# Expert weights in runs of 8192 bytes, with strided moving columns in the up product

## The chip, the cores and the metric

One core of a Trainium2 chip runs the whole program. The metric is the device time of one execution in microseconds; before the change its median over three runs is 1952.04 us (1950.11 to 1953.3).

## What is computed

The program computes four blocks over 256 tokens of 1024 features, in f32. The first block has two layers; each is a mixer (convolutions in the first, stick-breaking attention in the second), a layer norm, a mixture of experts and another layer norm. The second block (attention mixers and dense feed-forward parts) follows and is untouched here. The mixture of experts, which the change is about:

```python
g_logits = h @ rg_w + rg_b                   # 4 groups
grp = argmax(g_logits)
top_val, top_idx = top_k(e_logits[grp], 2)   # 2 of the group's 8 experts
weights = g_gate * softmax(top_val)
gate, up = split(rows_of_e @ w_up[e], 2)     # w_up[e]: 1024 x 1024
y = (silu(gate) * up) @ w_down[e]            # w_down[e]: 512 x 1024
out[tok] += y * weight
```

There are 32 experts in each of the two layers, and the kernel loads the weights of all of them: 4 MiB up and 2 MiB down for an expert.

## The kernel before

**The stages.** `tile_kernel` runs ten stages in order: convolutions (0), experts (1), stick-breaking attention (2), experts (3), and the second block (4 to 9). All weights are cut into items of at most 1 MiB, in the order of their use, in the list `items` (lines 125 to 176). `pump` (line 195) takes the next item as soon as a free buffer of 128 x 2048 f32 is usable for it and issues one DMA for it on SP's queue (line 205). `take` hands an item to its user, `done` gives the buffer back and pumps again. There are 7 buffers for all stages, 6 and 4 more while the first block runs, and 3 for the expert stages alone, so up to 20 items are under way or wait for TensorE when an expert stage begins. Items are loaded strictly in order: behind an expert stage's 192 items come those of the next mixer.

**An expert's items** (lines 137 to 143). The up weights are four items, the down weights two. `rows` (line 69) puts row 128 k + p of a matrix on partition p, at place k, and an item holds two places: on every partition two separate rows of 4096 bytes.

**The expert stage** (`moe`, from line 829). `router` picks the experts and leaves, for each token and expert, a place among 32 (`CAP`) in `rt["pos"]`. `gather_mm` (line 822) multiplies 128 features of `x` by a one-hot matrix, so that a group of tokens comes out with features on partitions; `gathered` brings the result through the layer norm's gain and bias (`put`, line 845) into `xgs`. The gain and bias stand on partitions in `fvec` (line 320), which `vector_loads` (line 322) makes by eight transposes. For expert e the loop then calls `up(e)`, `down(e - 1)` and `turn(e)`:

- `up` (line 882) has for each of its four items two places k, and for each of those four matmuls (j = 0 to 3). The stationary operand is the 32 gathered tokens, the moving one 256 columns of the weights: 128 gate columns and 128 up columns. Result j goes to partitions 32 j to 32 j + 31, so the four matmuls use the four column groups of the array. An f32 matmul leaves two records in the trace, so an up product has 8 x 4 x 2 = 64.
- `turn` (line 899) transposes the 32 x 512 hidden values, folded as 128 x 128, so that hidden units lie on partitions.
- `down` (line 906) does the same with the two down items, 32 records, and ScalarE copies the result out (line 921).

Every fourth expert `combine` (line 924) adds four experts' results into the accumulators. The next group of experts is gathered at places 5 and 6 of a group, and the first half of the first group inside `router`, ahead of the first up product.

Line 1658, in the attention of stage 7, multiplies the weights of a small compressor by `kps[n][:, :, l:l + 113:8]`: 75 moving columns with a step of eight elements. It is not changed.

Of the kernel before, what the change touches and what calls it, by code (L numbers as in the profile page):

```python
# [10 lines left out]
F32 = mybir.dt.float32  # L11
# [23 lines left out]
LN_MIX_G, LN_MIX_B, LN_FFN_G, LN_FFN_B, NORM = 0, 2, 4, 6, 8  # L35
# [33 lines left out]
def rows(ap):  # L69
    return ap.rearrange("(k p) n -> p k n", p=128)  # L70


@with_exitstack
def tile_kernel(ctx: ExitStack, tc: tile.TileContext, A, out, first=0, last=9):
    nc = tc.nc
    V, S, G, T, Q = nc.vector, nc.scalar, nc.gpsimd, nc.tensor, nc.sync
    NA, NB, NC, ND = 7, 6, 4, 3

    const = ctx.enter_context(tc.tile_pool(name="const", bufs=1))
# [7 lines left out]
    def bank():  # L87
        return psum.tile([128, 512], F32, name="ps", tag="ps")
# [4 lines left out]
    items, halves = [], []  # L93

    def dense(view, kind):
        items.append(view)
        i = len(items) - 1
        if kind in ("cols4", "cols2"):
            k = int(kind[4])
            n = 1024 // k  # L100
            for j in range(2):
                halves.append((i, (k, n), lambda t, j=j, k=k, n=n: t.rearrange("p (k n) -> p k n", k=k)
                               [:, :, j * n:(j + 1) * n]))
        elif kind == "feat":
            for m in range(2):
                halves.append((i, (8, 128), lambda t, m=m: t.rearrange("p (k n) -> p k n", k=8)
                               [:, :, m * 128:(m + 1) * 128]))
        elif kind == "gate":
            halves.append((i, (8, 112), lambda t: t[:, 0:896].rearrange("p (k n) -> p k n", k=8)))
        else:  # L110
            k, n = {"tok": (4, 256), "row": (1, 1024)}[kind]
            for j in range(2):
                halves.append((i, (k, n), lambda t, j=j, k=k: t[:, j * 1024:(j + 1) * 1024]
                               .rearrange("p (k n) -> p k n", k=k)))

    def cols(w, c0, n=256):
        return rows(w)[:, :, c0:c0 + n]

    def out_items(w, pairs=False):
        for j in range(0 if pairs else 2):  # L120
            dense(rows(w)[:, 0:4, j * 512:(j + 1) * 512], "cols4")
        for k in range(0 if pairs else 4, 8, 2):
            dense(rows(w)[:, k:k + 2, :], "cols2")
# [3 lines left out]
    for s in range(first, last + 1):  # L127
        stage_half[s] = len(halves)
        if s == 0:
            for i in range(2):  # L130
                dense(cols(A["even_w_in"][0], 2048 + 256 * i), "feat")
                dense(cols(A["even_w_in"][0], 1536 + 256 * i), "feat")
            for i in range(2):
                for c in (512, 1024, 0):
                    dense(cols(A["even_w_in"][0], c + 256 * i), "feat")
            out_items(A["even_w_out"][0])
        elif s in (1, 3):
            moe_items[s] = len(items)
            for e in range(NE):
                for k in range(4):  # L140
                    items.append(rows(A["expert_w_up"][s // 2, e])[:, 2 * k:2 * k + 2, :])
                for k in range(2):
                    items.append(rows(A["expert_w_down"][s // 2, e])[:, 2 * k:2 * k + 2, :])
        elif s == 2:
            for hg in range(4):
                dense(cols(A["odd_w_qkv"][0], 256 * hg), "feat")
                dense(cols(A["odd_w_qkv"][0], 1024 + 256 * hg), "feat")
                dense(cols(A["odd_w_qkv"][0], 2048 + 256 * hg), "tok")
            out_items(A["odd_w_o"][0])
        elif s == 4:  # L150
            for hg in range(4):
                for j in range(3):
                    dense(cols(A["w_in_ab_2"][0], (hg // 2) * 1536 + (hg % 2) * 256 + 512 * j), "tok")
            out_items(A["w_out_ab_2"][0], True)
        elif s in (5, 8):
            for f in range(NF + 1):
                if f < NF:
                    dense(cols(A["w_ffn_gate_2"][s // 7], 256 * f), "feat")
                    dense(cols(A["w_ffn_up_2"][s // 7], 256 * f), "feat")
                if f:  # L160
                    dense(rows(A["w_ffn_down_2"][s // 7])[:, 2 * f - 2:2 * f, :], "row")
        elif s in (6, 9):
            dense(rows(A["w_ple_proj_2"][s // 9]), "row")
            for u in range(4):
                dense(cols(A["w_ple_gate_2"][s // 9], 256 * u), "feat")
        else:
            w = A["w_in_nsa_2"][0]
            for j, n in enumerate(("k", "v")):
                dense(cols(w, 1024 + 256 * j), "tok")
            for n in ("k", "v"):  # L170
                items.append(A[f"cmp_{n}_w1_2"][0].rearrange("(l p) n -> p l n", p=128))
            for c in (1536, 2048):
                dense(cols(w, c), "tok")
            dense(cols(w, 2496, 112), "gate")
            for c in (0, 256, 1792, 2304, 512, 768):
                dense(cols(w, c), "tok")
            out_items(A["w_out_nsa_2"][0], True)
# [32 lines left out]
    def take(i):  # L210

        pump()
        t = raw[i]
        return t

    def done(i):
        if i not in taken:
            taken.add(i)
            free.append(where[i])
            pump()  # L220
# [75 lines left out]
    x = const.tile([128, 2, D], F32, name="x")  # L296
# [17 lines left out]
    ident = const.tile([128, 128], F32, name="ident")  # L314
# [4 lines left out]

    fvec = const.tile([128, 8, 14], F32, name="fvec")  # L320

    def vector_loads(vr):
        lo, hi = (0 if first < 4 else 8), (14 if last > 3 else 8)
        for j, n in enumerate(("ln_mix_g", "ln_mix_b", "ln_ffn_g", "ln_ffn_b", "norm_mix_2", "norm_ffn_2",
                               "norm_ple_2")):
            if lo <= 2 * j < hi:
                Q.dma_start(vr[2 * j:2 * j + 2, :], A[n])
        if lo:
            V.memset(vr[0:8, :], 0.0)

        def go():
            ps = bank()
            for k in range(8):
                T.transpose(ps[:, k * 14:k * 14 + hi], vr[0:hi, k * 128:(k + 1) * 128], ident[:hi, :hi])
            V.tensor_copy(fvec[:, :, 0:hi], ps[:, 0:112].rearrange("p (k n) -> p k n", k=8)[:, :, 0:hi])
        return go

    def fv(j):
        return lambda k: fvec[:, k, j:j + 1]
# [201 lines left out]
    def conv_mix():  # L541
        mp = rt["pool"]
        with tc.tile_pool(name="cm", bufs=1, reuse_waits="tile") as cp:
# [9 lines left out]
            Q.dma_start(fvr[36:37, :], A["even_norm_b_b"])  # L553
            pump(1)
            vectors = vector_loads(vr)
            prep = router_loads(0)
            pump()
# [165 lines left out]
    def router(mp):  # L723
# [59 lines left out]
        def first():  # L783
            place(0)
            warm(8)
            gather_mm(pg, 0, dsp[:, 0, 0:4])
# [35 lines left out]
    def gather_mm(ps, c, dsp):  # L822

        for k in range(8):
            T.matmul(ps[k // 4][:, k % 4 * 128:k % 4 * 128 + 128], x[:, c, k * 128:(k + 1) * 128],
                     dsp.rearrange("p e s -> p (e s)"), start=k % 4 == 0 and c == 0, stop=c == 1,
                     skip_group_check=True)

    def moe(layer):
        stage = 2 * layer + 1  # L830
        with tc.tile_pool(name="wd", bufs=ND, reuse_waits="tile") as wd, \
# [5 lines left out]
            router(mg)  # L837
            base = moe_items[stage]
            acc = [bank() for _ in range(4)]
            gain, bias = fv(LN_MIX_G + layer), fv(LN_MIX_B + layer)  # L840
            xgs, y4s, hts = {}, {}, {}
            dsp = rt["dt"][:, 0:512].rearrange("p (c e s) -> p c e s", c=2, e=8)
            dwt = rt["dt"][:, 512:].rearrange("p (q t) -> p q t", q=2)
# [38 lines left out]
            def up(e):  # L882
                g, el = divmod(e, 8)
                pu = bank()
                for kq in range(4):
                    i = base + 6 * e + kq
                    w = take(i).rearrange("p (k a j f) -> p k a j f", k=2, a=2, j=4)
                    for kk in range(2):
                        k = 2 * kq + kk
                        r = xgs[g][k // 4][:, k % 4, el * CAP:(el + 1) * CAP]  # L890
                        for j in range(4):
                            T.matmul(pu[32 * j:32 * j + 32, 0:256], r, w[:, kk, :, j, :], start=k == 0, stop=k == 7)  # L892
                    done(i)
                hs = mg.tile([128, 128], F32, name="hs")
                S.activation(hs, pu[:, 0:128], AF.Silu)  # L895
                V.tensor_tensor(out=hs, in0=hs, in1=pu[:, 128:256], op=OP.mult)  # L896
                hts[e] = hs
# [1063 lines left out]
    if 7 in stage_half:  # L1961
        j = halves[stage_half[7]][0]
# [51 lines left out]
```

## Time and profile before

| | |
|---|---|
| median of 3 runs | 1952.04 us |
| the profiled execution | 1952.0 us, span 1950.3 us |
| PE busy | 1638.0 us, 84% |
| PE weight loads busy | 1241.2 us, 64% |
| DVE, ACT, POOL busy | 40%, 35%, 10% |
| mean granted TensorE clock | 0.900 |
| DMA | 236570 packets, 559.04 MB, mean 287 GB/s |
| packets under 8 KB | 236408 |

Busy time is the union of an engine's instructions; matmuls are pipelined and their ends are modelled. The slices are fortieths of the span, 48.8 us each; a digit is the busy share in tenths. The DMA share is the mean busy share of the core's 16 DMA engines, and it can pass 1 where packets overlap. [...]

### The profile page before, as it was taken

The page shows a single profiled execution, that of the slowest core. Times are in us where ns is not written, and L with a number is a line of the kernel's source. Part 1 is how long each engine was busy: PE and PEld are TensorE (multiplying, and loading weights), DVE is VectorE, ACT ScalarE, POOL GpSimd, SP SyncE. Part 2 cuts the span into 40 slices and gives each one's busy share as a digit, 9 for nine tenths or more (in the row PEclk, how much of TensorE's full clock was granted, in tenths as well). Part 3 has the DMA queues.
Part 4 walks back from the last instruction along what each step waited for, and adds up shares of the span by engine and source line. Part 5 has one row for each costly group of instructions (what it writes and reads, how often), then busy time and mean ns, then how long its engine had stood idle before and what let it go on. Part 6 is the DMA issues. An engine that isn't in the chain of part 4 may idle for free. (4 is left out here: it accounts for less than half of the span.)

```text
span 1950.3 us, 34572 instructions
## 1 busy us (share of the span) xinstructions
PE 1638.0 (84%) x14717; PEld 1241.2 (64%) x14717; DVE 781.6 (40%) x1569; ACT 681.3 (35%) x1299; POOL 196.3 (10%) x152
## 2 busy tenths in 40 slices
PE   7769767667668999767657778999999998999998
PEld 7756423224226986323324225999999997799998
DVE  5873100001104663100001004666655857666557
ACT  3423111111114663211111114655444646654445
POOL 4721000000001000000000002111000412110001
PEclk9889878778878999977778788999999999999999
DMA  9549999999999659999999999545555463145550
GB/s 299 213 143 394 418 419 418 418 420 418 418 419 349 241 182 362 418 420 419 418 418 419 419 419 310 161 154 179 180 186 178 140 207 112 55 136 195 192 176 23
DMA packets 236570, 559.04 MB, mean 287 GB/s; under 512 B 15563, under 2 KB 124938, under 8 KB 236408
## 3 DMA queue, kind: packets, MB, share of 16 engines
q1 hardware_dynamic: 226520, 551.59, 74.3%
q10 hardware_dynamic: 9264, 4.97, 0.9%
q8 instruction: 119, 1.95, 0.4%
q14 instruction: 43, 0.35, 0.1%
q0 software_dynamic: 624, 0.18, 0.0%
HBM read 555.55 MB, written 1.15 MB: 285 GB/s over the span
## 5 line engine op out<-in xcount | busy, mean ns | idle before, releaser
L892 PE MATMUL ps<-w,xg 128*32 128x256 f32 x4096 | 362.3, 493 | 235.8 <-DMA w<-in_expert_w_up_dram 231.5
L892 PEld LDWEIGHTS ps<-w,xg 128*32 128x32 f32 x4096 | 134.7, 132 | 445.5 <-DMA w<-in_expert_w_up_dram 266.2
L251 DVE TENSOR_TENSOR wl<-w,wh 128x1024 fp32r<-128x1024 f32 x231 | 281.2, 1226 | 157.2 <-ACT wh L240 153.9
L240 ACT ACTIVATE wh<-w 128x1024 fp32r<-128x1024 f32 x273 | 283.5, 1051 | 90.5 <-PE ps L401 60.1
L896 DVE TENSOR_TENSOR hs<-hs,ps 128x128 f32<-128x128 f32 x64 | 18.4, 288 | 631.6 <-ACT hs L895 631.6
L400 PE MATMUL ps<-xh,wh 128*128 128x256 f32 (+1 forms) x840 | 237.1, 282 | 0.0
L402 PE MATMUL ps<-xh,wl 128*128 128x256 f32 (+1 forms) x840 | 236.3, 281 | 0.8 <-DVE wl L251 0.8
L401 PE MATMUL ps<-xl,wh 128*128 128x256 f32 (+1 forms) x840 | 236.6, 282 | 0.4 <-DVE xl L1218 0.3
L895 ACT ACTIVATE hs<-ps 128x128 f32<-128x128 f32 x64 | 17.8, 278 | 591.9 <-PE ps L892 587.2
L251 POOL TENSOR_TENSOR wl<-w,wh 128x1024 fp32r<-128x1024 f32 x42 | 115.5, 2764 | 996.2 <-ACT wh L240 996.2
L402 PEld LDWEIGHTS ps<-xh,wl 128*128 128x128 f32 (+1 forms) x840 | 159.2, 189 | 1.2 <-DVE wl L251 1.2
L401 PEld LDWEIGHTS ps<-xl,wh 128*128 128x128 f32 (+1 forms) x840 | 159.2, 189 | 1.2 <-DVE xl L1218 1.2
L400 PEld LDWEIGHTS ps<-xh,wh 128*128 128x128 f32 (+1 forms) x840 | 159.2, 190 | 0.0
L914 PE MATMUL ps<-w,ht 128*32 128x256 f32 x2048 | 144.9, 432 | 0.0
L921 ACT ACTIVATE y<-ps 32x256 f32<-32x256 f32 x256 | 96.0, 375 | 119.9 <-PE ps L914 113.8
L914 PEld LDWEIGHTS ps<-w,ht 128*32 128x32 f32 x2048 | 74.5, 128 | 67.6 <-issue 35.7
L402 PE MATMUL ps<-wh,xl 128*128 128x256 f32 x352 | 100.4, 285 | 5.0 <-DVE xl L1218 5.0
L400 PE MATMUL ps<-wh,xh 128*128 128x256 f32 x352 | 102.2, 290 | 1.5 <-ACT xh L1215 1.5
L401 PE MATMUL ps<-wl,xh 128*128 128x256 f32 x352 | 99.6, 283 | 0.0
L401 PE MATMUL ps<-al,wh 128*128 128x256 f32 x352 | 99.1, 281 | 0.0
L400 PE MATMUL ps<-ah,wh 128*128 128x256 f32 x352 | 99.0, 281 | 0.0
L402 PE MATMUL ps<-ah,wl 128*128 128x256 f32 x352 | 99.0, 281 | 0.0
(403 smaller groups left out, 2883.5 us busy)
## 6 DMA issues: line engine op xcount, KB each, us to landing
w<-in_expert_w_up_dram SPq DMA_DIRECT2D x256, 1024.0 KB
w<-in_expert_w_down_dram SPq DMA_DIRECT2D x128, 1024.0 KB
w<-in_w_ffn_gate_dram SPq DMA_DIRECT2D x22, 1024.0 KB
w<-in_w_ffn_up_dram SPq DMA_DIRECT2D x22, 1024.0 KB
w<-in_w_ffn_down_dram SPq DMA_DIRECT2D x22, 1024.0 KB
w<-in_odd_w_qkv_dram SPq DMA_DIRECT2D x12, 1024.0 KB
w<-in_w_in_ab_dram SPq DMA_DIRECT2D x12, 1024.0 KB
w<-in_w_in_nsa_dram SPq DMA_DIRECT2D x10, 1024.0 KB
```

The costliest lines, as they stand in the source:

```text
L240: S.activation(hv, src, AF.Copy)
L251: eng.tensor_tensor(out=lv, in0=src, in1=hv.bitcast(F32), op=OP.subtract)
L400: T.matmul(ps, lh, rh, start=start, stop=False, **kw)
L401: T.matmul(ps, lh, rl, start=False, stop=False, **kw)
L402: T.matmul(ps, ll, rh, start=False, stop=stop, **kw)
L892: T.matmul(pu[32 * j:32 * j + 32, 0:256], r, w[:, kk, :, j, :], start=k == 0, stop=k == 7)
L895: S.activation(hs, pu[:, 0:128], AF.Silu)
L896: V.tensor_tensor(out=hs, in0=hs, in1=pu[:, 128:256], op=OP.mult)
L914: T.matmul(pd[32 * c:32 * c + 32, 0:256], hts[e][:, 32 * j:32 * j + 32], w[:, jj, c * 256:(c + 1) * 256], start=j == 0, stop=j == 3)
L921: S.activation(y4s[q][32 * ee:32 * ee + 32, c * 256:(c + 1) * 256], pd[32 * c:32 * c + 32, 0:256], AF.Copy)
```

## The change

The expert weights are cut by a new view, `runs`, which puts rows 8 p to 8 p + 7 of an up matrix (4 p to 4 p + 3 of a down matrix) on partition p. An item still holds two places, but they are now adjacent in memory: one run of 8192 bytes on each partition. Three things follow from it. Feature 8 p + k of the tokens has to lie on partition p at place k, so `gather_mm` takes every eighth feature as its stationary operand, and the gain and bias are needed in that order too (`runvec`). And hidden unit 4 p + j has to lie on partition p for the down product, so the up product's result j takes every fourth column of the weights.

```diff
+def runs(ap):
+
+    return ap.rearrange("(p k) n -> p k n", p=128)
...
                 for k in range(4):
-                    items.append(rows(A["expert_w_up"][s // 2, e])[:, 2 * k:2 * k + 2, :])
+                    items.append(runs(A["expert_w_up"][s // 2, e])[:, 2 * k:2 * k + 2, :])
                 for k in range(2):
-                    items.append(rows(A["expert_w_down"][s // 2, e])[:, 2 * k:2 * k + 2, :])
+                    items.append(runs(A["expert_w_down"][s // 2, e])[:, 2 * k:2 * k + 2, :])
...
+    runvec = const.tile([128, 8, 4], F32, name="runvec") if first < 4 else None
...
             V.tensor_copy(fvec[:, :, 0:hi], ps[:, 0:112].rearrange("p (k n) -> p k n", k=8)[:, :, 0:hi])
+            if not lo:
+                ps = bank()
+                for k in range(8):
+                    T.transpose(ps[:, k * 4:k * 4 + 4], vr[0:4, k::8], ident[:4, :4])
+                V.tensor_copy(runvec.rearrange("p k n -> p (k n)"), ps[:, 0:32])
...
-            T.matmul(ps[k // 4][:, k % 4 * 128:k % 4 * 128 + 128], x[:, c, k * 128:(k + 1) * 128],
+            T.matmul(ps[k // 4][:, k % 4 * 128:k % 4 * 128 + 128], x[:, c, k::8],
...
-            gain, bias = fv(LN_MIX_G + layer), fv(LN_MIX_B + layer)
+            gain, bias = [lambda k, j=j + layer: runvec[:, k, j:j + 1] for j in (LN_MIX_G, LN_MIX_B)]
...
-                    w = take(i).rearrange("p (k a j f) -> p k a j f", k=2, a=2, j=4)
+                    w = take(i).rearrange("p (k a f j) -> p k a j f", k=2, a=2, j=4)
```

## Rows read from the trace of the kernel before

**Rows 1.** The page's 40 slices: busy tenths, granted clock, DMA share, rate.

```profile
PE   7769767667668999767657778999999998999998
...
PEclk9889878778878999977778788999999999999999
DMA  9549999999999659999999999545555463145550
GB/s 299 213 143 394 418 419 418 418 420 418 418 419 349 241 182 362 418 420 419 418 418 419 419 419 310 161 154 179 180 186 178 140 207 112 55 136 195 192 176 23
```

**Rows 2.** Windows; columns as in the first line, x counts instructions.

```profile
core 0: us, PE busy (x) PEld busy (x) DVE busy (x) ACT busy (x) POOL busy (x), PEclk, DMA share, GB/s
...
175.00:592.00 417.00, 298.06 (x3153) 137.30 (x3151) 35.44 (x102) 63.00 (x173) 3.46 (x6) 0.80 1.03 418
181.00:186.00 5.00, 5.00 (x96) 2.85 (x88) 0.44 (x2) 1.41 (x5) 0.00 (x0) 1.00 1.02 415
700.00:745.00 45.00, 45.00 (x308) 37.02 (x306) 28.06 (x67) 18.84 (x31) 1.10 (x2) 1.00 0.67 248
745.00:1183.00 438.00, 311.33 (x3374) 148.14 (x3377) 40.57 (x125) 72.33 (x192) 0.00 (x0) 0.81 1.02 416
```

**Rows 3.** Waits, 175 to 592 and 745 to 1183 us: total us, times, longest.

```profile
PE ps L892 <- DMA w<-in_expert_w_up_dram: 113.2, 92, 5.1
...
PE ps L892 <- DMA w<-in_expert_w_up_dram: 117.8, 93, 6.0
```

**Rows 4.** Timeline from 300 us: start, length, engine, line, operation, idle time before.

```profile
300.24 1.94 PE L892 MATMUL ps<-w,xg 128*32 128x256 f32 x16 [0.46 <-DMA w<-in_expert_w_up_dram]
300.67 0.20 PEld L892 LDWEIGHTS ps<-w,xg 128*32 128x32 f32 x4 [0.23 <-issue]
301.10 0.20 PEld L892 LDWEIGHTS ps<-w,xg 128*32 128x32 f32 x4 [0.23 <-issue]
...
302.81 1.69 PE L892 MATMUL ps<-w,xg 128*32 128x256 f32 x16 [0.63 <-DMA w<-in_expert_w_up_dram]
```

**Rows 5.** Timeline from 181 us, where an expert's weights had landed.

```profile
180.75 3.66 PE L892 MATMUL ps<-w,xg 128*32 128x256 f32 x64
...
184.23 1.91 PE L914 MATMUL ps<-w,ht 128*32 128x256 f32 x32
```

**Rows 6.** DMA issues of the page.

```profile
w<-in_expert_w_up_dram SPq DMA_DIRECT2D x256, 1024.0 KB
w<-in_expert_w_down_dram SPq DMA_DIRECT2D x128, 1024.0 KB
```

**Rows 7.** DMA view: 622 to 626, 526.0 to 526.5, 300 to 301 us; packets, MB, share.

```profile
DMA packets 1524, 1.54 MB, mean 386 GB/s; under 512 B 16, under 2 KB 1524, under 8 KB 1524
...
q14 instruction: 1, 0.01, 3.9%
...
q1 hardware_dynamic: 109, 0.42, 103.2%
```

**Rows 8.** PE's groups by line: operands, count, busy us, mean ns, idle before.

```profile
L892 PE MATMUL ps<-w,xg 128*32 128x256 f32 x4096 | 362.3, 493 | 235.8 <-DMA w<-in_expert_w_up_dram 231.5 <-DVE x L950 3.3 <-issue 1.0
...
L825 PE MATMUL ps<-dt,x 128*128 128x128 f32 x512 | 60.5, 276 | 0.4 <-DVE dt L780 0.4
L927 PE MATMUL ps<-y,dt 128*128 128x512 f32 x128 | 57.6, 592 | 0.0
...
L901 PE MATMUL ps<-ident,hs 128*128 128x128 f32 x64 | 21.3, 333 | 1.4 <-DVE hs L896 1.4
...
L334 PE MATMUL ps<-ident,scr 14*128 14x14 f32 x8 | 0.8, 230 | 0.0
```

**Rows 9.** Line 1658's records (ns min/median/max, first and last start), and its window.

```profile
L1658 PE MATMUL ps<-kpk,w x32: 297/317/320, 1570.7 to 1574.9; 128*128 128x75 f32 x32
...
1570.60:1575.20 4.60, 4.60 (x36) 4.60 (x35) 0.63 (x1) 0.24 (x1) 0.00 (x0) 1.00 0.01 4
```

**Rows 10.** Timeline ahead of the second expert stage's first up product.

```profile
745.38 2.05 PE L825 MATMUL ps<-dt,x 128*128 128x128 f32 x16 [0.18 <-DVE dt L780]
```

## The prediction, made before the change was built

> **What bounds the kernel now.** I read the sliced page first [rows 1]. The DMA line stands at 9 and about 418 GB/s in two long plateaus, slices 3 to 11 and 16 to 23, and the granted TensorE clock sags to 0.7 to 0.8 in just those slices. Cutting at the plateaus [rows 2] gives two stretches, 175 to 592 us and 745 to 1183 us, 417 + 438 = 855 us together, with DMA share 1.02 to 1.03 and 416 to 418 GB/s. They are the two expert stages: each loads 192 items of 1 MiB (six per expert), and an item takes 1048576 / 418e9 = 2.51 us, an expert 15.05 us. PE is busy about 71% of both. Which of the two ends last is in the waits [rows 3]: the up products wait 113.2 us and 117.8 us there for their own weights, in some 92 waits each. One item in the timeline [rows 4] shows it: a burst of 16 matmul records of 1.94 us, then 0.63 us until the next item lands. [...] Where the weights had already landed [rows 5], all 64 records of an expert's up product take 3.66 us at granted clock 1.00 [rows 2]. So in 855 of 1950 us the weight stream sets the pace, and PE has room.
>
> The profiled execution took 1952.0 us for its span of 1950.3 us, the median of the runs is 1952.04 us; the sum below is made against 1952.0.
>
> **Part 1: runs of 8192 bytes.** The 384 expert items [rows 6] keep their size and their issues (one per item, on SP, in the same order); each is cut into 128 runs of 8192 bytes in place of 256 of 4096. No row shows an 8192-byte packet on this queue, so I bound the saving from two sides. From rates: the stretch that loads 1024-byte packets alone runs at 386 GB/s [rows 7], 16 x 1024 / 386 = 42.4 ns per packet on one of 16 engines; 4096-byte packets at 418 GB/s take 156.8 ns. That is 38.1 ns per KB and 4.3 ns per packet, so 8192 bytes would take 309.3 ns against 2 x 156.8 = 313.6: 1.4%, or 12 us of 855. From packet times: a half microsecond in a plateau holds one 8192-byte packet, of the instruction queue, at 3.9% of 16 engines, 0.039 x 16 x 500 = 312 ns [rows 7]; in another microsecond 103 packets of 4096 bytes (0.42 MB) take 1.032 x 16 x 1000 / 103 = 160 ns each. 312 against 320 is 2.7%, or 23 us; it is the upper end, because shares above 1 say that packets already overlap a little. I take 2.0%, between them, as neither row is nearer: **17 us**.
>
> [...]
>
> **Part 2: the up products' moving columns.** The 4096 matmul records of the up product [rows 8] keep their number and width (256 columns) but read every fourth element. The nearest row with a strided moving operand is the compressor's product at line 1658, 75 columns with a step of eight elements [rows 9]: 32 records start within 1570.7 to 1574.9 us, (4.2 us / 31) 135 ns apart, 317 ns each, at granted clock 1.00. Contiguous ones are faster though wider: 118 ns apart for 128 columns at line 825 (60.5 us / 512), at mean 276 ns [rows 8]. So strided columns cost at most 135 / 75 = 1.8 ns each; the up product's cost 3.66 us x 4 / (64 x 256) = 0.89 ns. Lower end: no change, 3.66 us per expert. Upper end: all four column groups take turns for 1.8 ns, 16 x 4 x 256 x 1.8 = 29.5 us. I take 1.8 ns with the four groups side by side, as they are now, **7.4 us per expert**: that row is the only one with a stride.
>
> What hides it? Per expert at full clock [rows 5, 8]: down 1.91, combine 57.6 / 64 = 0.90, gather 60.5 / 64 = 0.95, turning the hidden rows 0.33: 4.1 us, with 7.4 that is 11.5 us of an expert's new 14.75 us of loading. PE stays ahead, at some 78% instead of 71%; a busier PE should show a higher granted clock. The cover is gone when the up product needs over 14.75 - 4.1 = 10.6 us, 2.9 times today's.
>
> [...]
>
> **Part 3: the gather and the vectors.** The gather's stationary operand becomes `x[:, c, k::8]`. Its records, loads included, are 118 ns apart now [rows 8]; no row has a strided stationary read. Below: nothing. Above: line 1658's pace, 128 x 1.8 = 230 ns, 112 ns more per load, 0.9 us per expert under the weight stream. Uncovered is only the first gather, with 16 records on the path to the first up product of a stage [rows 10]: 16 x 112 = 1.8 us at most; half of that, 0.9 us, as the ends are equally far. In the second stage the DMA engines are at share 0.67 just before [rows 2], because all buffers are full, so the first item freed sets when loading restarts; at 7.4 us the first quarter of the first up product ends 0.9 us later. Together **+1.8 us**; bounds 0 to 7, twice both delays at their ends with some waiting for buffers. `vector_loads` gains eight transposes and a copy; the eight now there take 0.8 us [rows 8], PE in the first stage is 70 to 90% busy [rows 1]; between 0 and 0.8 I take **+0.4 us**. The gain and bias come from `runvec` instead of `fvec`: same instructions, nothing. No queue gets another instruction, and no wait is added.
>
> **Sum:** 1952.0 - 17 + 1.8 + 0.4 = **1937 us**. What the earlier end of a stage shifts, the next stages follow; the prefetch of the next dense weights comes on the same queue, also earlier.
>
> **The rivals.**
> *The up product becomes the bound.* Four strided streams read the same 128 partitions at once, and line 1658 shows one alone. If two at a time get through, the up product takes 16 x 2 x 256 x 1.8 = 14.7 us, an expert 14.7 + 4.1 = 18.8 us against 15.05, so 64 x 3.75 = 240 us more: 2192 us. If all take turns, 33.6 us, some 1200 us more. It decides above 10.6 us. For it: no row shows four strided streams, and 1.8 ns is already twice the contiguous pace. Against it: the four contiguous streams run side by side, 57 ns per record where single ones of 256 columns would need four times as long. Chance 0.17.
> *The stream does not get faster.* The descriptors may still be cut at 4096 bytes, or the plateau may be held by what bytes cost rather than packets; then Parts 2 and 3 remain, about +2 us: 1954 us. For it: between 1024 and 4096 bytes a packet the rate gained only 8%, so most of the cost goes by bytes. Against it: the instruction queue's 8192 bytes do move as one packet, in less than two of 4096. Chance 0.13.
> *The small costs win.* The stream gains only its lower end or less, and the strided loads on the path, or PE at its lower clock falling behind the stream, cost 15 us and more: 1956 to 1975 us. Chance 0.05.
>
> **How the numbers follow.** Forecast 0.65 for 1937 us; its own range, 23 us saved with nothing lost to 12 us saved with 8 lost, is 1929 to 1948. The range for 8 in 10 adds the second rival and part of the third: 1927 to 1962; the first rival is left out. A measurement tells 0.2% (4 us) from no change: faster 0.65; same 0.13, all of the second rival; slower 0.17 + 0.05 = 0.22.
>
> **What would show it.** Right: packets of 8 KB and more on the page rise by 49152, the plateaus go to 424 to 430 GB/s at the same share, an item takes about 2.46 us, the up product about 7.4 us where its weights had landed, the granted clock in the plateaus rises over 0.85, and the up product still waits for its weights, though less. Wrong: the waits for up weights vanish and PE is busy all through the plateaus (the first rival), or 418 GB/s stay with the packet count unchanged (the second). The forecast also falls if the up product keeps 3.66 us; the time would then be 1 to 2 us lower.

## The result, and the profile after

The changed kernel takes 1966.7 us (median of 4 runs, 1964.51 to 1968.88) against 1951.76 us before in the same session: ratio 1.0078, 95% interval 1.0064 to 1.0092. It is slower by some 15 us, where 15 us less was forecast.

The page of the changed kernel, its slices and the two groups that the change touches (in the order of [rows 1] and [rows 8]):

```profile
PE   7769999979888999998979878999999998999998
...
PEclk9889999999999999999999999999999999999999
DMA  9638999999999757999999999544555463235550
GB/s 290 228 140 329 413 421 420 421 421 420 420 421 333 257 194 301 391 421 420 420 421 421 421 421 347 167 140 162 194 187 185 146 197 106 69 131 197 184 182 23
DMA packets 187418, 559.04 MB, mean 285 GB/s; under 512 B 15563, under 2 KB 124938, under 8 KB 138104
...
L904 PE MATMUL ps<-w,xg 128*32 128x256 f32 x4096 | 490.3, 631 | 80.2 <-DMA w<-in_expert_w_up_dram 74.7
...
L837 PE MATMUL ps<-dt,x 128*128 128x128 f32 x512 | 125.3, 402 | 0.4 <-DVE dt L792 0.4
```

Three things are to be seen. The packets fell from 236570 to 187418, by 49152: the long runs are there. The plateaus rose, but only from 418 to 420 or 421 GB/s. And the slices in which they begin fell: 394 to 329 and 418 to 413 in slices 3 and 4, 362 to 301 and 418 to 391 in slices 15 and 16. Slice 0, where no expert weight has been used yet and 11264 of 15105 packets are of 512 bytes to 2 KB, fell too, from 299 to 290. From slice 3 on the granted clock, a share of full speed, is at 0.9 or more in every slice, the plateaus among them (mostly 0.7 or 0.8 before), and TensorE is now busy 92% of the span.

The timeline at the start of the first expert stage shows the two stepped reads:

```profile
153.82 4.08 PE L837 MATMUL ps<-dt,x 128*128 128x128 f32 x16
...
158.99 4.08 PE L837 MATMUL ps<-dt,x 128*128 128x128 f32 x16 [0.18 <-DVE dt L792]
...
163.01 7.43 PE L904 MATMUL ps<-w,xg 128*32 128x256 f32 x64
...
171.42 7.44 PE L904 MATMUL ps<-w,xg 128*32 128x256 f32 x64
...
178.66 1.92 PE L926 MATMUL ps<-w,ht 128*32 128x256 f32 x32
```

An up product takes 7.43 us instead of 3.66 [rows 5], a gather of 16 records 4.08 instead of 2.05 [rows 10]. And the windows of the same stretch (columns as in [rows 2]; the last three are granted clock, DMA share and GB/s):

```profile
160.00:165.00 5.00, 5.00 (x33) 3.63 (x37) 1.37 (x4) 1.51 (x4) 0.00 (x0) 1.00 0.01 3
165.00:170.00 5.00, 5.00 (x49) 1.56 (x41) 0.00 (x0) 0.00 (x0) 0.00 (x0) 1.00 0.80 292
170.00:175.00 5.00, 4.30 (x39) 1.42 (x38) 2.68 (x16) 3.26 (x5) 0.00 (x0) 1.00 0.91 329
...
190.00:195.00 5.00, 4.48 (x40) 1.76 (x44) 0.46 (x1) 0.60 (x1) 0.00 (x0) 1.00 0.70 251
```

In the kernel before the same four windows read:

```profile
160.00:165.00 5.00, 4.30 (x79) 2.54 (x75) 1.86 (x12) 2.24 (x5) 0.00 (x0) 1.00 0.85 297
165.00:170.00 5.00, 5.00 (x84) 3.32 (x73) 1.55 (x8) 2.43 (x6) 0.00 (x0) 1.00 1.04 416
170.00:175.00 5.00, 2.94 (x27) 2.75 (x25) 1.96 (x5) 1.87 (x5) 0.00 (x0) 1.00 1.01 410
...
190.00:195.00 5.00, 5.00 (x50) 2.44 (x46) 1.50 (x5) 1.78 (x5) 0.51 (x1) 0.99 1.03 420
```

All buffers are full then, and loading restarts only when TensorE gives one back: SP issues the next expert item at 165.07 us, at 159.81 us before. The first up product now starts later (163 instead of 158.7 us) and gives buffers back more slowly, and the engines that load stand idle from 160 to 165 us (share 0.01) and again for a third of the time from 190 to 195 us (share 0.70).

So two questions were open: why the plateau rose by 0.6% and not by the 1.4 to 2.7% that the prediction had bounded, and how much of the loss belongs to the stage starts.

### The profile page after: what moved, and what is told of

The parts are those of the page before. It is cut to its first block, busy times and chain, and to the rows that moved or that the text cites. A ratio compares the mean times of both kernels' runs of the same rounds, so it can differ in the third digit from the quotient of the medians.

```text
span 1964.9 us, 34589 instructions
## 1 busy us (share of the span) xinstructions
PE 1805.7 (92%) x14725; PEld 1304.3 (66%) x14725; DVE 781.6 (40%) x1570; ACT 681.4 (35%) x1299; POOL 196.4 (10%) x152
## 2 busy tenths in 40 slices
DMA packets 187418, 559.04 MB, mean 285 GB/s; under 512 B 15563, under 2 KB 124938, under 8 KB 138104
## 5 line engine op out<-in xcount | busy, mean ns | idle before, releaser
L904 PE MATMUL ps<-w,xg 128*32 128x256 f32 x4096 | 490.3, 631 | 80.2 <-DMA w<-in_expert_w_up_dram 74.7
L837 PE MATMUL ps<-dt,x 128*128 128x128 f32 x512 | 125.3, 402 | 0.4 <-DVE dt L792 0.4
L837 PEld LDWEIGHTS ps<-dt,x 128*128 128x128 f32 x512 | 124.1, 336 | 2.1 <-DVE dt L792 2.1
L926 PE MATMUL ps<-w,ht 128*32 128x256 f32 x2048 | 123.8, 381 | 0.0
```

The lines of the kernel that those rows point to most:

```text
L926: T.matmul(pd[32 * c:32 * c + 32, 0:256], hts[e][:, 32 * j:32 * j + 32], w[:, jj, c * 256:(c + 1) * 256], start=j == 0, stop=j == 3)
```

## The experiments

**First set: each part alone.** The theory then was that the long runs are worth only what the changed plateau shows, and that the stage starts cost the rest.

The loads alone, on the kernel before:

```diff
-                    items.append(rows(A["expert_w_up"][s // 2, e])[:, 2 * k:2 * k + 2, :])
+                    items.append(runs(A["expert_w_up"][s // 2, e])[:, 2 * k:2 * k + 2, :])
...
-                    items.append(rows(A["expert_w_down"][s // 2, e])[:, 2 * k:2 * k + 2, :])
+                    items.append(runs(A["expert_w_down"][s // 2, e])[:, 2 * k:2 * k + 2, :])
```

> The loads of the change alone: the expert items are cut into runs of 8192 bytes, while the gather and the up product read as before (so features and hidden units meet the wrong weight rows, which costs no time). Theory: the change loses at the start of each expert stage, where TensorE frees buffers later, and its runs of 8192 bytes give only what the plateau of the changed kernel shows, 421 against 418 GB/s, 0.6% of 855 us; this kernel then takes 1952 - 5 = 1947 us, its first up products start where they did before, and its plateau stands at 420 to 421 GB/s. Rival: the strided reads of TensorE hold back the writes of the stream, so the runs are worth more without them; the plateau then stands at 424 to 428 GB/s and the time is 1938 to 1942 us.

Measured: 1935.73 us, ratio 0.9924 (0.9911 to 0.9937), 15 us less. The theory falls. The rival's plateau comes out, and the time is 2 us under the rival's range. One plateau window of this kernel, 300 to 400 us (columns as in [rows 2]):

```profile
300.00:400.00 100.00, 72.68 (x747) 34.17 (x747) 7.98 (x24) 16.03 (x44) 0.00 (x0) 0.79 1.01 425
```

425 GB/s instead of 418: the long runs are worth what the prediction gave them, and something in the changed kernel takes more than half of it away.

The stepped gather alone:

```diff
-            T.matmul(ps[k // 4][:, k % 4 * 128:k % 4 * 128 + 128], x[:, c, k * 128:(k + 1) * 128],
+            T.matmul(ps[k // 4][:, k % 4 * 128:k % 4 * 128 + 128], x[:, c, k::8],
```

> The strided stationary operand of the gather alone (every eighth feature), all else as before, so the gathered features meet the wrong weight rows. Theory: two gathers of 4.1 us in place of 2.05 us stand ahead of the first up product of each stage while all buffers are full, so each stage ends some 4 us later, and a little more through the third gather: 1960 to 1963 us. Rival: the stream makes up for the late start, or the gather was hidden by the router's vector work: 1952 to 1954 us.

Measured: 1958.72 us, ratio 1.0041 (1.0028 to 1.0054), 8 us more: near the theory, a little below it. The first up product starts at 162.38 us instead of 158.68 us.

The stepped up product alone:

```diff
-                    w = take(i).rearrange("p (k a j f) -> p k a j f", k=2, a=2, j=4)
+                    w = take(i).rearrange("p (k a f j) -> p k a j f", k=2, a=2, j=4)
```

> The up product's moving columns with a step of four alone, loads and gather as before, so the down product meets the wrong hidden units. Theory: the up product takes 7.4 us where its weights have landed, the first buffer of a stage is freed 0.9 us later and the next ones at half the pace, so each stage loses 1 to 3 us, while the plateau stays at 418 GB/s: 1954 to 1958 us. Rival: the strided reads hold back the stream in the plateau, which falls below 416 GB/s: over 1958 us.

Measured: 1956.1 us, ratio 1.0027 (1.0017 to 1.0038), 5 us more, with plateaus at 418 and 419 GB/s: the theory holds. So the rival of the first run, that stepped reads hold the stream back, is not seen with runs of 4096 bytes.

The change for experts 8 to 31 alone (core of the edit):

```diff
-                    items.append(runs(A["expert_w_up"][s // 2, e])[:, 2 * k:2 * k + 2, :])
+                    items.append((runs if e > 7 else rows)(A["expert_w_up"][s // 2, e])[:, 2 * k:2 * k + 2, :])
...
-            T.matmul(ps[k // 4][:, k % 4 * 128:k % 4 * 128 + 128], x[:, c, k::8],
+            T.matmul(ps[k // 4][:, k % 4 * 128:k % 4 * 128 + 128], x[:, c, k::8] if late else
+                     x[:, c, k * 128:(k + 1) * 128],
```

> The change for the experts 8 to 31 of each stage alone; the first eight experts, which are computed while the buffers are full, are loaded, gathered and read as before. Theory: the starts of the stages are those of before, and 144 of 192 items a stage come at 421 in place of 418 GB/s: 2 x 144 x 2.5 us x 0.6% = 4 us saved, 1948 us. Rival: the cost lies in the higher load of TensorE through the whole stage, so it comes back with three quarters of the experts: 1956 us or more.

Measured: 1953.45 us, ratio 1.001 (1.000 to 1.0019). Neither: the starts are as before (415 GB/s from 165 to 170 us, 416 before), but the 4096-byte items of the first group then load at 407 GB/s, and the 8192-byte items behind them at 420 and 421. One window of this kernel, which holds 4096-byte items, and the same of the kernel before:

```profile
175.00:225.00 50.00, 48.06 (x559) 31.05 (x559) 8.04 (x24) 11.17 (x31) 3.45 (x6) 0.97 1.03 407
...
175.00:225.00 50.00, 45.90 (x605) 26.77 (x603) 7.96 (x24) 12.50 (x34) 3.46 (x6) 0.97 1.03 418
```

So even the 4096-byte items were slower here, by 11 GB/s.

**Second set: what holds the plateau at 421?** Candidates were the stepped reads with long runs, a busier TensorE, or the stepped gather.

Two adjacent rows in blocks of 256 rows, which needs a step of two only (against the changed kernel):

```diff
-    return ap.rearrange("(p k) n -> p k n", p=128)
+    return ap.rearrange("(h p k) n -> p h k n", p=128, k=2)
...
-            T.matmul(ps[k // 4][:, k % 4 * 128:k % 4 * 128 + 128], x[:, c, k::8],
+            T.matmul(ps[k // 4][:, k % 4 * 128:k % 4 * 128 + 128], x[:, c, 256 * (k // 2) + k % 2:256 * (k // 2) + 256:2],
...
-                    w = take(i).rearrange("p (k a f j) -> p k a j f", k=2, a=2, j=4)
+                    w = take(i).rearrange("p (k a h f j) -> p k a h j f", k=2, a=2, h=2, j=2)
```

> Runs of 8192 bytes with a step of two: every item is one block of 256 weight rows, two adjacent rows on a partition, so the gather takes every second feature and the up product every second column; the result is the reference's. [...] Rival: any step costs: the up product takes over 5 us, the gather over 3 us, the plateau stays at 421 GB/s and the time is 1950 us or more.

Measured: 1947.49 us, ratio 0.9983 (0.9974 to 0.9992). Half of the rival: the plateau stays at 420 GB/s, but gather (2.15 us) and up product (3.85 us) are close to their contiguous pace (2.05 and 3.66 us), and the time is under the rival's, though 12 us over that of the loads alone.

Each matmul of the up product twice, contiguous, with long runs (on the kernel with the loads alone; core of the edit):

```diff
-                    for kk in range(2):
+                    for kk in (0, 0, 1, 1):
```

> The loads alone (runs of 8192 bytes, contiguous reads, wrong weight rows), with each matmul of the up product done twice, so that TensorE reads as long as in the changed kernel but without a step. Theory: the plateau lost 425 to 421 GB/s to the stepped reads themselves; here it stays at 425 GB/s, and only the slower start of a stage costs, as in the run with the stepped up product alone: 1939 to 1943 us. Rival: it lost it to a busier TensorE, whatever it reads: plateau 420 to 421 GB/s, 1947 us or more.

Measured: 1946.35 us, ratio 0.9973 (0.9963 to 0.9984), with the plateau at 425 GB/s. A busier TensorE does not hold the stream back: it is busy 85.2 of the 100 us from 300 to 400 us, 72.7 with the loads alone, and both load at 425 GB/s. The time came out above the theory, near the rival, so it decides by the plateau alone.

Long runs and stepped up product, gather as before (on the kernel with the loads alone):

```diff
-                    w = take(i).rearrange("p (k a j f) -> p k a j f", k=2, a=2, j=4)
+                    w = take(i).rearrange("p (k a f j) -> p k a j f", k=2, a=2, j=4)
```

> The changed kernel with a contiguous gather (features meet the wrong weight rows) and without the eight transposes. Theory: runs of 8192 bytes and a stepped up product together hold the plateau at 421 GB/s, which costs 855 us x 1% = 8 us on top of the stepped up product's own 5 us: 1947 to 1951 us. Rival: the gather's stepped weight loads hold the stream back; without them the plateau is at 425 GB/s and the time 1939 to 1943 us.

Measured: 1940.2 us, ratio 0.9946 (0.9931 to 0.9962), plateau 425 and 426 GB/s. The theory falls; the rival, the gather, fits so far.

Long runs for the up weights alone, so a stepped gather and a contiguous up product:

```diff
-                    items.append(runs(A["expert_w_down"][s // 2, e])[:, 2 * k:2 * k + 2, :])
+                    items.append(rows(A["expert_w_down"][s // 2, e])[:, 2 * k:2 * k + 2, :])
...
-                    w = take(i).rearrange("p (k a f j) -> p k a j f", k=2, a=2, j=4)
+                    w = take(i).rearrange("p (k a j f) -> p k a j f", k=2, a=2, j=4)
```

> Runs of 8192 bytes for the up weights alone, so the gather is stepped and the up product is contiguous; the result is the reference's. Theory: two thirds of the items gain, the plateau stands at 422 to 423 GB/s, 10 us of the 15 us are saved and the gather costs its 8 us, the transposes up to 2 us: 1949 to 1953 us. Rival: the stepped gather also holds back the stream: plateau under 420 GB/s, 1955 us or more.

Measured: 1964.98 us, ratio 1.0071 (1.0056 to 1.0086), plateau 416 and 417 GB/s, under that of the kernel before although two thirds of its items have long runs. The rival's numbers came out, but the gather can't be the reason: alone, it left the plateau at 418 and 419 GB/s.

What divides the lower plateaus from the others is none of the reads. Those at 425 (or 418 with short runs) were made from the kernel before; those at 421 or less were made from the changed one, and all of these have the tile `runvec`, 128 x 8 x 4 f32. It takes 128 bytes a partition among the constants, ahead of the weight buffers, so that every buffer behind it lies 128 bytes higher. In the allocation of the program 13 of the 20 weight buffers start on a multiple of 256 bytes before the change, and 128 bytes behind one after it; the other seven start 32 bytes ahead of a multiple before, and 96 bytes behind one after. That would also reach slice 0.

**Third set: the place of the buffers.** The kernel before with an unused tile:

```diff
     fvec = const.tile([128, 8, 14], F32, name="fvec")
+    const.tile([128, 32], F32, name="pad")
```

> The kernel before with one unused constant tile of 128 bytes a partition, the size of the new gain and bias tile, so that every weight buffer lies 128 bytes higher in SBUF; nothing else differs. Theory: the changed kernel's plateau is at 421 and not 425 GB/s because of where the buffers lie, not because of what TensorE reads; here the plateau falls from 418 to 410 to 415 GB/s, the first 48.8 us load at about 290 instead of 299 GB/s, and the time is 1958 to 1968 us. Rival: the place of the buffers does not matter and something else that these kernels share is at work (the eight transposes, the order of the program): 1950 to 1953 us, plateau 418 GB/s.

Measured: 1971.63 us, ratio 1.0102 (1.0086 to 1.0117): 20 us more, and below the plateau that was expected, in its window from 300 to 400 us:

```profile
300.00:400.00 100.00, 64.95 (x706) 31.29 (x710) 6.82 (x21) 13.68 (x38) 0.00 (x0) 0.84 1.03 409
```

409 instead of 418 GB/s, from 128 bytes that nobody reads, and slice 0 falls from 299 to 287 GB/s. The theory holds, with the time a little over and the plateau a little under its range.

The changed kernel with 128 more bytes, 256 in all (`gg` takes the place of `gm`, to make room):

```diff
     runvec = const.tile([128, 8, 4], F32, name="runvec") if first < 4 else None
+    const.tile([128, 32], F32, name="pad")
...
-            ge, gg, den = small("ge", 4), small("gg"), small("den")
+            ge, gg, den = small("ge", 4), gm, small("den")
```

> The changed kernel with 128 more unused bytes of constants, so that the buffers lie 256 bytes higher than before the change instead of 128 (one small tile of the router shares another's place to make room). Theory: the plateau comes back to 425 GB/s and the changed kernel keeps its stepped gather and up product only: the 1940 us of runs and stepped up product, 8 us for the gather and up to 2 us for the transposes, 1948 to 1952 us. Rival: stays at 420 to 421 GB/s and 1963 us or more.

Measured: 1956.62 us, ratio 1.0024 (1.0015 to 1.0033), 10 us less than the changed kernel. The plateau is back, in its window from 300 to 400 us:

```profile
300.00:400.00 100.00, 94.62 (x823) 44.70 (x819) 8.28 (x25) 17.52 (x48) 0.00 (x0) 1.00 1.01 425
```

The time is 5 us over the theory's range: the stepped gather and up product together cost more than each alone (below).

The kernel with a step of two, padded in the same way (against that kernel):

```diff
     runvec = const.tile([128, 8, 4], F32, name="runvec") if first < 4 else None
+    const.tile([128, 32], F32, name="pad")
...
-            ge, gg, den = small("ge", 4), small("gg"), small("den")
+            ge, gg, den = small("ge", 4), gm, small("den")
```

> The kernel with a step of two (correct result) with the same 128 more unused bytes. Theory: plateau 425 GB/s, contiguous pace of gather and up product, 1936 to 1939 us, faster than both kernels. Rival: the plateau stays at 420 to 421 GB/s and the time at 1945 to 1949 us.

Measured: 1938.4 us, ratio 0.9931 (0.9918 to 0.9945), 14 us less than before. The theory holds, and this version beats both the kernel before and the changed one. Its plateau window (columns as in [rows 2]):

```profile
300.00:400.00 100.00, 71.74 (x747) 33.76 (x739) 7.99 (x24) 15.43 (x43) 0.00 (x0) 0.82 1.01 425
```

And its timeline at the start of the first expert stage, to be set beside that of the changed kernel above:

```profile
155.01 2.15 PE L838 MATMUL ps<-dt,x 128*128 128x128 f32 x16
...
158.25 2.15 PE L838 MATMUL ps<-dt,x 128*128 128x128 f32 x16 [0.18 <-DVE dt L793]
...
160.34 3.85 PE L905 MATMUL ps<-w,xg 128*32 128x256 f32 x64
```

A gather of 16 records takes 2.15 us instead of 4.08 and the first up product starts at 160.34 us instead of 163.01, with the long runs' full plateau of 425 GB/s behind it.

The kernel before, with 64 unused bytes instead of 128:

```diff
     fvec = const.tile([128, 8, 14], F32, name="fvec")
+    const.tile([128, 16], F32, name="pad")
```

> The kernel before with an unused constant tile of 64 bytes a partition instead of 128: 13 of the 20 weight buffers then start 64 bytes behind a multiple of 256 bytes, where they start on a multiple of 256 before the change and 128 bytes behind one in the changed kernel. Theory: every start away from a multiple of 256 costs a packet some 4 ns, so the plateau is again at 407 to 410 GB/s and the time at 1968 to 1974 us. Rival: half the distance costs half, or only the distance of 128 bytes costs: plateau 413 GB/s or more, 1962 us or less.

Measured: 1973.15 us, ratio 1.0109 (1.0092 to 1.0126), as the theory has it. Its window from 300 to 400 us:

```profile
300.00:400.00 100.00, 69.86 (x699) 32.44 (x698) 7.09 (x22) 15.05 (x42) 0.00 (x0) 0.76 1.02 408
```

**The same traces, item by item.** A move of 128 bytes moves everything behind it, what TensorE reads too. What the stream alone pays can be told apart inside one kernel, because only 13 of the 20 buffers start on a multiple of 256 bytes there. The traces hold the time at which each of the 16 engines finished its part of an item, and the program's allocation says where that item's buffer starts. The mean time from one expert item's landing to the next one's, in us, for the items in the plateaus of the first and the second stage (standard errors up to 0.006):

| kernel | buffers on a multiple of 256 | the other buffers |
|---|---|---|
| before | 2.48, 2.48 | 2.57, 2.56 |
| before, 128 bytes more | none | 2.57, 2.57 |
| loads alone | 2.45, 2.45 | 2.51, 2.50 |
| changed | none | 2.50, 2.50 |
| changed, 128 bytes more | 2.46, 2.45 | 2.51, 2.50 |

So it is the start of the buffer that an item is written to: items into the seven buffers off a multiple of 256 already take 0.08 us longer in the kernel before, and after the move all items take that long. TensorE's reads do not tell them apart: an up product whose weights had landed takes 3.66 us before and after the move. The sums fit: 246 of the 384 expert items go to the 13 buffers, and 246 x 0.09 = 22 us with short runs, 246 x 0.05 = 12 us with long ones, against 20 and 11 us measured.

## Why the prediction was wrong

**The account.** By the ratios, times 1951 us: the long runs -15 (loads alone, 0.9924); the stepped up product with them +4 (0.9946); the stepped gather and the eight transposes on top +15 (padded, 1.0024); the place of the buffers +11 (changed kernel, 1.0078). Together +15. The prediction had -17, +1.8, +0.4 and nothing.

**Part 1, the long runs: right.** 425 for 418 GB/s is 1.7%, 14 of 855 us, and the loads alone measured 15 us; 2.0% had been taken, between 1.4 and 2.7%. That the changed kernel shows only 0.6% is another part's doing.

**Part 2, the up product: its size right, its cover half right.** 7.4 us was forecast from line 1658, 7.43 us came, with the four column groups side by side; so the first rival, with over 10.6 us, did not come. In the plateau the stream still covers it: in the long-run kernel with stepped columns the rate is 425 GB/s and up products still wait for their weights (56.0 and 57.4 us in the two plateaus). The step that failed is the cover per expert, "PE stays ahead": it was an average over a stage, and at its start, with every buffer full, loading goes at the pace at which TensorE frees buffers (in the kernel with the stepped columns alone 242 GB/s from 160 to 165 us, 297 before). The price was foreseen only as 0.9 us for the first buffer of the second stage; alone the stepped columns cost 5 us.

**Part 3, the gather: mis-sized, above its upper end.** The records of the gather come 245 ns apart (125.3 us / 512), 127 more than before, where 0 to 112 had been allowed and half taken. Both first gathers stand ahead of the first up product, not one of them: its start moves from 158.68 to 162.38 us in the kernel with the gather alone. The third gather, 7.8 us between the second and third up product, then leaves a hole with no buffer freed. Under contiguous up products loading lives through it (190 to 195 us: share 1.03 in the kernel with the gather alone); after stepped ones the share is 0.70, the padded kernel has 0.67 there, so the hole is not the buffers' place. The lines for the hole, the gather alone first, then the padded kernel:

```profile
190.00:195.00 5.00, 5.00 (x93) 2.82 (x89) 0.58 (x2) 1.32 (x4) 0.00 (x0) 1.00 1.03 419
...
190.00:195.00 5.00, 4.25 (x40) 1.88 (x44) 0.69 (x2) 0.60 (x1) 0.00 (x0) 0.66 0.67 251
```

That the stage starts hold the whole of this loss is in the windows of both starts, first of the loads alone, then of the padded kernel:

```profile
160.00:200.00 40.00, 37.24 (x552) 22.11 (x544) 9.07 (x36) 12.46 (x30) 0.74 (x2) 0.96 0.99 412
743.00:790.00 47.00, 41.22 (x588) 25.20 (x584) 9.50 (x36) 15.74 (x39) 0.00 (x0) 1.00 1.01 422
...
160.00:200.00 40.00, 37.24 (x306) 20.67 (x310) 6.88 (x28) 8.91 (x20) 0.00 (x0) 0.96 0.80 313
743.00:790.00 47.00, 44.06 (x319) 26.13 (x322) 10.20 (x47) 9.92 (x20) 0.00 (x0) 0.96 0.81 321
```

The padded kernel loads 4.0 and 4.7 MB less in them, which at 425 GB/s is 9 + 11 = 20 us; +4 and +15 were measured. The same sum gives 8 us for the gather alone (against the kernel before) and 4 us for the stepped columns with long runs, so the two cost some 8 us more together than apart; in the first stage the hole from 190 to 200 us is 2.6 us of that. The eight transposes are a small part: the padded kernel with a step of two has eight as well, and all of it costs 1.4 us over the loads alone (0.9931 against 0.9924).

**"The gain and bias come from `runvec`: same instructions, nothing": wrong, by 11 us.** Its instructions cost little: the padded kernel with a step of two has them too and stays within 1.4 us of the loads alone. Its 128 bytes moved the buffers that the stream writes to, and items into the 13 that left a multiple of 256 land 2.50 us apart, where they land 2.45 or 2.46 apart in the padded kernel. This is shown from both sides: 128 bytes alone make the kernel before slower by 20 us, and another 128 take 10 us off the changed kernel; and inside one kernel it is the items into buffers off a multiple of 256 that come later (2.57 against 2.48 us in the kernel before). An effect of this kind was in none of the rivals. "The stream does not get faster" had the right symptom, 418 to 421 GB/s, with another cause.

Of the signs named in advance, the packet count, the granted clock, the 7.4 us and the up products that wait less (27.4 and 36.1 us in the plateaus, from 113.2 and 117.8 [rows 3]) came out; the plateau of 424 to 430 GB/s did not.

The price of a step stands in these runs. A step of four f32 doubled the up product's time (7.43 against 3.66 us), a step of two left it nearly alone (3.85 us), and the gather of 16 records goes the same way (4.08, 2.15 and 2.05 us for steps of eight, two and one). No run has a step of three, and none shows why a step of four costs a factor of two and a step of two next to nothing.

## What to carry to other kernels

Before an expected gain in a stream is judged, look where its buffers start: a new constant ahead of them can move all of them, so give the comparison a control with the same bytes unused, and keep the buffers that loads are written to on multiples of 256 bytes (with 13 of 20 on one the plateau was 425 GB/s here with runs of 8192 bytes, with none 420). Where a layout needs a stepped read, choose the blocks so that the step is two and not four: here, in f32, that kept the long runs and nearly all of TensorE's pace (3.85 us an up product, 7.43 with a step of four). And cost a change at the start of a stage by itself; at the two starts of the padded kernel the buffers were full and the consumer, not the stream, set the pace (DMA share 0.80 and 0.81, against 0.99 and 1.01 with the loads alone).

## What the runs showed of the hardware that was not expected

The cost of the moved buffers went by packets and not by bytes here. At 418 and 409 GB/s a packet of 4096 bytes takes 16 x 4096 / 418 = 156.8 and 160.2 ns of an engine, 3.4 ns more; at 425 and 420 GB/s one of 8192 bytes takes 308.4 and 312.1 ns, 3.7 ns more. These are means over all buffers; by the landings a packet into a buffer off a multiple of 256 takes some 5 ns (4096 bytes) or 6 ns (8192 bytes) more than one into a buffer on it. So long packets lose half as much, 11 us and not 20. Starts 64 and 128 bytes behind a multiple of 256 cost the same (408 and 409 GB/s), the seven buffers that start 32 bytes ahead of one cost as much (2.56 against 2.57 us an item), and a move by 256 bytes cost nothing in the plateau (425 GB/s with it and without it). Why a start off the multiple costs this stays open.

The kernel before and the padded kernel with a step of two still pay for these seven buffers, to which 138 of the 384 expert items go. With all buffers on a multiple of 256 they would gain some 138 x 0.08 = 11 us and 138 x 0.05 = 7 us, an estimate from the landings that no run has tried.
